# A two-layer block with GELU on one core: when transposes and stores are given out on SP's queue

## The chip, the cores and the metric

The kernel runs on one core of a Trainium2 chip. The metric is the time of one execution on the device in microseconds (us), lower is better. Before: 1465.05 us, the median of three runs (1464.21 to 1468.51).

## The reference

```python
# x: (8, 1024, 1024) float32, w1: (1024, 4096), w2: (4096, 1024)
h = x @ w1
h = 0.5 * h * (1 + np.tanh(np.sqrt(2 / np.pi) * (h + 0.044715 * h ** 3)))
return (h @ w2).astype(np.float32)
```

## The kernel before

**Tiling.** The 8192 rows of x are taken in eight token blocks of 1024 rows (`sb` 0 to 7). Each runs a first multiplication (x by w1, GELU on ScalarE, result g) and a second (g by w2, result to `out`). Both are split into 2 x 2 blocks, named "11", "12", "21", "22", and are done with seven products in place of eight (the scheme of Strassen and Winograd): products 1, 2 and 3 take blocks of the weights as they are, 5, 6, 7 and 4 take sums of them (`W1_SUM`, `W_SUM`, listed in `SUMS`), and sums of x or g stand on the other side (`X_SUM`, and the jobs `g`). From block 2 on, a second level of the same scheme is used inside the products. Data are float16, accumulation is in float32 in PSUM.

**The stage in question** is the second multiplication of token block 0, `matmul2_made(0, ...)`. It computes what the later blocks will load ready-made, and stores it to DRAM: the four blocks of w2 (`keep`, into `w2_d`, shown as `w_d` in the profile), and for each operand m the sums that the second level needs (`split_jobs`, into `in_d[m]`). Its products run in the order 1, 2, 5, 6, 3, 7, 4, each in four quarters of 128 rows (sixteen matmuls each); product 3 is done with the second level, in seven steps.

**The order by hand.** After each quarter, `run((m, q))` looks into the table `FILL[0]` and does the jobs written there. The key `60` stands for product 6, quarter 0, and so on; `31` to `37` are the seven steps of product 3. The jobs: `g` sums of g; `wmn` piece n of the sum of w2 for product m (`make`); `pmn` the split sum n of operand m with its store to `in_d[m]`; `a` the inner sums of g; `x` and `q` the sums of x and of w1 for the next token block; `i` inner sums of w1. VectorE does them in this order, in between the sums that empty PSUM (`post`).

**Queues.** Most loads, and some stores, are issued on SP's queue (`nc.sync`, and `load_in_order`, which also fixes their place in the program's order); other stores, and copies that cast, are issued by POOL. Each queue issues in order: what stands first and waits holds up what stands behind it. A DMA of SP's queue also starts only when the eighth before it on that queue has landed.

**The next block's x.** During product 5, POOL starts eight copies of the next 1024 rows of x from float32 to float16 in DRAM (`x_cast`, buffer `xb`). `x_transpose` loads from that buffer with the transposing DMA into four tiles, in the order "22", "21", "12", "11", four transposes for each; SP's queue waits for the cast to land. `x_blocks` takes the four tiles.

**Who waits for what.** Tiles `u` come from a pool of 24, tiles `mu` from one of two, `gc` from one of four. The split sums p35 and p36 of operand 3 lie in `u` tiles, p37 and p34 in the two `mu` tiles. p25, p26, p27 and p24 of operand 2, which VectorE makes from the end of product 3 on, take the place of some of these once those have been read by TensorE and stored. Product 4 needs the sums w40 to w43, which come behind p27 and p24 on VectorE. The first multiplication of block 1 begins with the raw blocks of w1 that `MadeQuad(0, False, True)` loads, and with the transposed x.

In the profile, L1127 is the second level's matmul in the second multiplication, L1182 the one of a plain product there, L502 that of a plain product in the first, L719 that of the second level there. L142 is VectorE's addition or subtraction, L169 ScalarE's copy, L166 a DMA given out by `load_in_order`, L203 a load of w1's raw blocks, L836 and L848 stores of results, L1010 the store of a split sum.

Of the kernel before, what the change touches and what calls it, by code (L numbers as in the profile page):

```python
# [23 lines left out]
SUMS = tuple(W_SUM)  # L24
# [19 lines left out]
def slots(table):  # L44
# [4 lines left out]
    slots("""10:g60 p15;11:g61 p16;12:g62 p17;13:g63  # L49
    ;20:g50 w50 w51;21:g51 w52;22:w53 g52;23:g53 p14  # L50
    ;50:w60 w61;51:w62 w63;52:g30 g31;53:g32 g33
    ;60:p35 p36;61:a35 p37;62:a37 p34;63:a36
    ;31:w70;32:a33;33:w71;34:w72;35:w73;36:p25;37:p26
    ;70:p27 p24;71:w40 w41;72:w42 w43;73:x5;40:x7;41:x6;42:x3 q5 q6 q7 q4
    ;43:i2""".replace("\n    ", "")),
# [21 lines left out]
def kernel(  # L77
# [7 lines left out]
    nc = tc.nc  # L85
# [38 lines left out]
    in_d = {m: dram.tile([P, 4, NI // 2, OH // 2], DT, name=f"in_d{m}") for m in range(1, 8)}  # L124
# [5 lines left out]
    term = {b: m for m, b in W_TERM.items()}  # L130
# [7 lines left out]
    def unit(rows, cols):  # L138
        return up.tile([P, rows, cols], DT, name="u")

    def tt(out, in0, in1, op, pin=False):
        i = nc.vector.tensor_tensor(out=out, in0=in0, in1=in1, op=op)  # L142
        if pin:
            tc.keep_in_program_order(i)

    def w1_at(q, key):
        for (at, ks), d in w1_d.items():
            if at == q and key in ks:
                return d[:, :, ks.index(key), :]

    def w2_at(q, m):
        return w2_d[q // 2, m][:, :, q % 2, :]

    def halves(t):
        return t.rearrange("p (h k) n -> p h (k n)", h=2)
# [9 lines left out]
    def load_in_order(out, in_, **kw):  # L165
        return tc.keep_in_program_order(nc.sync.dma_start(out=out, in_=in_, **kw))  # L166
# [26 lines left out]
    class MadeQuad:  # L193


        def __init__(self, q, first, store):
            self.q, self.first, self.store = q, first, store
            self.raw = {b: unit(2 * KH, 2 * P) for b in BLOCKS}
            self.ops = {m: self.raw[b] for m, b in W_TERM.items()}
            if not first:  # L200
                queue = nc.sync
                for b in ("12", "11", "22", "21") if q else ("11", "21", "12", "22"):
                    queue.dma_start(out=halves(self.raw[b]), in_=w1_at(q, term.get(b, b)))  # L203

        def load(self):

# [156 lines left out]
    def x_blocks():  # L363
        return {b: unit(KH, HT) for b in ("22", "21", "12", "11")}
# [107 lines left out]
    def x_cast(s, after, rows=range(0, SB, P), xb=None):  # L472
        if xb is None:
            xb = xdram.tile([SB, H], DT, name="xb")
        with tc.issue_after(after.ins):
            for q in rows:
                nc.gpsimd.dma_start(out=xb[q:q + P, :], in_=x2[s * SB + q:s * SB + q + P, :])
        return xb
# [8 lines left out]
    def x_transpose(xb, dma, blocks=None, which=range(4)):  # L487
        blocks = blocks or x_blocks()
        for b, t in [list(blocks.items())[i] for i in which]:
            a, k = int(b[0]) - 1, int(b[1]) - 1  # L490
            for j in range(KH):
                dma(
                    t[:, j, :],
                    xb[a * HT:(a + 1) * HT, (k * KH + j) * P:(k * KH + j + 1) * P],
                    transpose=True,
                )
        return blocks
# [343 lines left out]
        rows = out2[r0:r0 + HT // 2, o0:o0 + OH // 2].rearrange("(i p) n -> p i n", p=P)  # L841
        return nc.sync.dma_start(out=rows, in_=src)

    def store_rows(sb, o, a, src, **kw):
        r0 = sb * SB + (int(o[0]) - 1) * HT + a * HT // 2
        o0 = (int(o[1]) - 1) * OH
        rows = out2[r0:r0 + HT // 2, o0:o0 + OH].rearrange("(i p) n -> p i n", p=P)
        return nc.gpsimd.dma_start(out=rows, in_=src, **kw)  # L848

    def matmul2_made(sb, g, keep_w1, xb):  # L850

# [23 lines left out]
        def keep(b):  # L875
            if sb == 0:
                for q in range(NI // QC):
                    load_in_order(w2_at(q, term.get(b, b)), raw[b][q])
# [3 lines left out]
        def make(m, q):  # L882
            if m not in sums:
                sums[m] = raw[over[m]] if m in over else [unit(2, HALF) for _ in range(NI // QC)]
            u, op, v = W_SUM[m]
            in0, in1 = (sums[b][q] if isinstance(b, int) else raw[b][q] for b in (u, v))
            tt(sums[m][q], in0, in1, op, True)
            if sb:
                n = 1 if q < 2 else 2
                nc.gpsimd.dma_start(out=w2_at(q, m)[:, :n], in_=sums[m][q][:, :n])  # L890
# [4 lines left out]
        def rows(t, q):  # L895
            return t[:, :, q * P:(q + 1) * P]

        s2, a, p5, t6, at = {}, {}, {}, {}, {}
# [3 lines left out]
        deep = {m: Inner(m, g[operands[m]]) for m in ((3,), (4,))[sb]}  # L902
        for m, d in deep.items():
            d.base, d.y = [], parts[m]
            d.rows = lambda r, t, o={3: "12", 4: "21"}[m]: store_rows(sb, o, r, t)

        def run(key):
            for job in FILL[sb].get(key, ()):
                kind, m, n = job[0], int(job[1]), int(job[2:] or 0)
                if kind == "g" and m == 6:  # L910
                    s2[n] = gcp.tile([P, NI, P], GT, name="gc")
                    tt(s2[n], rows(g["22"], n), rows(g["21"], n), SUB, True)
                elif kind == "g" and m == 5:
                    tt(rows(g["11"], n), s2[n], rows(g["11"], n), ADD, True)
                elif kind == "g":
                    tt(rows(g["12"], n), rows(g["12"], n), s2[n], SUB, True)
                elif kind == "w":
                    make(m, n)
                elif kind == "p":
                    splits[m][SUMS.index(n)]()  # L920
                elif kind == "a":
                    deep[m].make(n)
                elif kind == "x":
                    xs.make(m, pin=True)
                elif kind == "q":
                    quad.sum(m, pin=True)
                elif kind == "i" and sb:
                    xs.make_inner(m)
                elif kind == "i":
                    quad.inner_sums(m)  # L930
# [31 lines left out]
        for m, name, first in (  # L962
            (1, "a", True), (2, "b", True), (5, "c", True), (6, "a", False),
            (3, "c", False), (7, "a", False), (4, "a", False),
        ):
            if m in deep:
                deep[m].pieces = pieces(m)
                for n in deep[m].steps(deep[m].base):
                    if (m, n) == (4, 1):
                        quad = StoredHalf(0)  # L970
                    run((m, n))
                continue
            for q in range(NQ):
                if first:
                    banks[name].append(psum())
                bank = banks[name][q]
                matmuls2(bank, s2[q] if m == 6 else rows(g[operands[m]], q), pieces(m), first)
                post(m, q, bank)
                if (m, q) == (5, 0) and sb == 0:
                    xb = x_cast(sb + 1, nc.gpsimd.tensor_copy(out=pace, in_=p5[0][:, :2]))  # L980
                if (m, q) == ((5, 0) if sb else (6, 0)):
                    xs = XOps(x_transpose(xb, load_in_order))
                if (m, q) == (6, 3):
                    keep("22")
                if (m, q) == (7, 0) and sb == 0:
                    quad = MadeQuad(0, False, True)
                if (m, q) == (1, NQ - 1) and sb == 0:
                    sums[5] = [unit(2, HALF) for _ in range(NI // QC)]
                    for t in sums[5]:
                        act_copy(t[:, 0, :1], warm)  # L990
                    bring("22", act_copy, True)
                    keep("21")
                    keep("12")
                run((m, q))
        return xs, [quad]

    def split_jobs(m, pieces, t):

        def operand(v, h):
            if isinstance(v, int):  # L1000
                return t[v][:, h * QC:(h + 1) * QC, :]
            k, b = int(v[0]) - 1, int(v[1]) - 1
            return chunks(pieces()[2 * k + h])[:, b]

        def make(n):
            u, op, v = W_SUM[n]
            t[n] = (mp.tile([P, NI // 2, OH // 2], DT, name="mu") if n in (7, 4) and m != 4 else unit(NI // 2, OH // 2))
            for h in range(2):
                tt(t[n][:, h * QC:(h + 1) * QC, :], operand(u, h), operand(v, h), op, True)
            (nc.sync if m == 3 else nc.gpsimd).dma_start(out=in_d[m][:, SUMS.index(n)], in_=t[n])  # L1010

        return [lambda n=n: make(n) for n in SUMS]

# [186 lines left out]
    def matmul2(sb, g, early, nxt):  # L1200
        end = sb == NSB - 1
        into = {}

        def out(o, **kw):
            return lambda a, t: store_rows(sb, o, a, t, **kw)

        operands = {1: "11", 2: "12", 5: "11", 6: "22", 7: "21", 3: "12"}
        products = {m: Inner(m, g[b]) for m, b in operands.items()}
# [72 lines left out]
    xs, quads = first.xs, [first.quad]  # L1281
    g_late = None
    for sb in range(NSB):
        if sb < 2:
            g, nxt = matmul1(xs, sb, quads, first if sb == 0 else None)
            xs, quads = matmul2_made(sb, g, None if sb else quads[-1].keep_raw, nxt)
# [3 lines left out]
        xs = nxt  # L1290
# [30 lines left out]
```

## Time and profile before

| | |
|---|---|
| median of three runs | 1465.05 us |
| profiled execution | 1467.82 us |
| its span in the trace | 1466.0 us |
| TensorE busy | 1449.4 us (99%) |
| VectorE busy | 1207.9 us (82%) |
| ScalarE busy | 712.2 us (49%) |
| POOL busy | 587.4 us (40%) |
| mean DMA rate | 314 GB/s |
| granted TensorE clock, mean | 0.997 |

The page's table in 40 slices of 36.65 us shows where the span is not full: the first slices cover block 0, whose stage in question lies from 112 to 218 us.

```
PE   9999979999999999999999999999999999999998
DVE  5657749858698898889898898988989889888887
PEclk9999989999999999999999999999999999999999
DMA  9999899898799999999999999999999999986594
```

The stretches below are taken from the trace, with the time that TensorE was busy, the mean share of time in which the 16 DMA engines were busy, and what they moved.

| from, to (us) | what runs on TensorE | TensorE busy (us) | DMA share | GB/s |
|---|---|---|---|---|
| 150.0 to 168.4 | products 5 and 6 | 18.40 of 18.40 | 1.03 | 280 |
| 168.4 to 193.4 | products 3 and 7 | 25.00 of 25.00 | 0.60 | 136 |
| 193.4 to 202.1 | nothing | 0.03 of 8.70 | 1.01 | 382 |
| 202.1 to 218.5 | product 4 | 16.37 of 16.40 | 1.02 | 367 |
| 218.5 to 275.0 | block 1, first multiplication | 56.20 of 56.50 | 0.98 | 364 |
| 275.0 to 280.0 | the same | 5.00 of 5.00 | 0.07 | 29 |

How to read the rows of the profile: a row of the timeline gives start, length, engine, line, operation, output and input tiles, and in brackets how long the engine had been idle before it and what released it. "SPq" is SP's queue of DMAs, and its lengths are those of issuing; a DMA lands later. A row of the stretches gives the stretch, its length, then the busy time of TensorE, its weight loads, VectorE, ScalarE and POOL with the number of instructions, and last the granted TensorE clock, the DMA share and GB/s. The chain of waits goes back from the last instruction to what released it each time.

### The profile page before, as it was taken

Reading aid. Unit: us, or ns where it says so; the run is one execution under the profiler, and the core shown is the slowest. Engines: PE = TensorE matmul, PEld = TensorE weight load, DVE = VectorE, ACT = ScalarE, POOL = GpSimd, SP = SyncE. Lnnn points to the kernel's source line nnn. Section 1 sums busy time; section 2 is a strip of 40 time slices with the busy share of each in tenths; the row PEclk is TensorE's granted clock in tenths of the full one; section 3 lists DMA queues with packets and bytes.
Section 4 is the critical chain, followed back from the end, with each engine's and each line's share of the span. In section 5 each row is a group of like instructions: output and inputs, shape, how many; then the busy total and the mean of one; then the engine's idle time right before and its main releaser. Section 6 shows DMA issues by size and latency. Waiting matters only on the chain.

```text
span 1466.0 us, 28909 instructions
## 1 busy us (share of the span) xinstructions
PE 1449.4 (99%) x10731; PEld 1049.3 (72%) x10731; DVE 1207.9 (82%) x2019; ACT 712.2 (49%) x1460; POOL 587.4 (40%) x602
## 2 busy tenths in 40 slices
PE   9999979999999999999999999999999999999998
PEld 5444634444577788778887788777887778877887
DVE  5657749858698898889898898988989889888887
ACT  5665105641158621785228841388225872268621
POOL 1542113222359500793018820388005960068400
PEclk9999989999999999999999999999999999999999
DMA  9999899898799999999999999999999999986594
GB/s 316 344 354 377 235 306 368 287 324 247 274 397 250 280 365 375 332 251 315 361 349 328 239 363 338 367 294 226 388 357 353 264 262 372 358 332 232 209 405 162
DMA packets 199116, 460.13 MB, mean 314 GB/s; under 512 B 75200, under 2 KB 80320, under 8 KB 198080
## 3 DMA queue, kind: packets, MB, share of 16 engines
q1 hardware_dynamic: 178208, 375.45, 74.5%
q0 software_dynamic: 20768, 82.85, 17.4%
q8 instruction: 84, 1.38, 0.4%
q14 instruction: 56, 0.46, 0.1%
HBM read 370.15 MB, written 102.76 MB: 323 GB/s over the span
## 4 chain that ended last, share of the span: by engine, by line
PE 96%; SPq 1%; DMA 1%; DVE 1%; issue 0%; ACT 0%; DVEq 0%
PE ps L1127 36%; PE ps L502 26%; PE ps L719 23%; PE ps L1182 11%; SPq L166 1%; PE ps L435 1%; DMA u<-in_d 1%; DVE u L142 0%; DMA u<-in_x_dram 0%; PE ps L412 0%; DMA in_d<-u 0%; DVE mu L142 0%; ACT u L169 0%; DVE tmp L142 0%; PE ps L370 0%
## 5 line engine op out<-in xcount | busy, mean ns | idle before, releaser
L169 ACT COPY tmp<-ps 128x512 f32<-128x512 f32 (+1 forms) x528 | 263.8, 540 | 238.9 <-PE ps L502 143.8
L502 PE MATMUL ps<-u 128*128 128x512 f16 x1472 | 343.2, 379 | 0.3 <-DVE tmp L142 0.3
L1127 PE MATMUL ps<-u,gc 128*128 128x256 f16 x2704 | 308.8, 273 | 0.8 <-DMA u<-in_d 0.8
L1127 PEld LDWEIGHTS <-gc 128*128 128x128 f16 x2816 | 275.5, 98 | 32.9 <-DMA u<-in_d 1.0
L142 DVE TENSOR_TENSOR u<-u 128x2048 f16<-128x2048 f16 (+3 forms) x292 | 221.9, 803 | 47.0 <-DMA in_d<-u 14.9
L142 DVE TENSOR_TENSOR tmp<-tmp,ps 128x256 f32<-128x256 f32 (+1 forms) x368 | 197.1, 544 | 71.5 <-PE ps L719 30.6
L719 PEld LDWEIGHTS <-u 128*128 128x128 f16 x2096 | 205.1, 98 | 57.3
L502 PEld LDWEIGHTS <-u 128*128 128x128 f16 x1472 | 144.1, 98 | 141.6 <-issue 0.9
L848 POOL DMA_DIRECT2D out_dram<-u x50 | 36.8, 735 | 515.5 <-DVE u L142 495.4
L1127 PE MATMUL ps<-u,g 128*128 128x256 f16 x2000 | 234.8, 273 | 0.0
L1127 PEld LDWEIGHTS <-g 128*128 128x128 f16 x2112 | 206.6, 98 | 24.3
L719 PE MATMUL ps<-u 128*128 128x256 f16 x1372 | 221.1, 273 | 0.0
L515 ACT ACTIVATE g<-tmp 128x512 f16<-128x512 f32 x282 | 174.2, 641 | 57.5 <-DVE tmp L142 56.6
L169 ACT COPY ps<-ps 128x256 f32<-128x256 f32 (+1 forms) x208 | 95.4, 458 | 219.3 <-PE ps L1127 219.3
L142 DVE TENSOR_TENSOR ps<-tmp,ps 128x256 f32<-128x256 f32 x444 | 181.5, 426 | 17.3 <-PE ps L719 9.4
L169 ACT COPY u<-ps 128x512 f32<-128x512 f32 (+1 forms) x114 | 66.2, 587 | 180.7 <-PE ps L1127 146.9
L142 DVE TENSOR_TENSOR u<-u,ps 128x512 f32<-128x512 f32 x174 | 118.5, 684 | 40.9 <-ACT u L169 20.9
L1182 PE MATMUL ps<-u,g 128*128 128x512 f16 x640 | 141.5, 384 | 8.7 <-DVE u L142 8.7
L515 ACT ACTIVATE g<-ps 128x512 f16<-128x512 f32 x230 | 137.9, 601 | 24.7 <-PE ps L719 15.2
L771 POOL TENSOR_TENSOR tmp<-tmp 128x512 f32<-128x512 f32 x96 | 122.2, 1275 | 41.8 <-DVE tmp L142 31.5
L142 DVE TENSOR_TENSOR tmp<-ps,tmp 128x512 f32<-128x512 f32 x126 | 86.6, 690 | 48.1 <-PE ps L502 40.3
L1182 PEld LDWEIGHTS <-g 128*128 128x128 f16 x640 | 63.2, 99 | 86.1 <-issue 12.5
(72 smaller groups left out, 1572.3 us busy)
## 6 DMA issues: line engine op xcount, KB each, us to landing
u<-w_d SPq DMA_DIRECT2D x347, 512.0 KB, 8.9
u<-in_d SPq DMA_DIRECT2D x162, 512.0 KB, 9.3
out_dram<-u POOLq DMA_DIRECT2D x50, 512.0 KB, 6.9
gc<-in_w_dram SPq DMA_DIRECT2D x48, 512.0 KB, 6.5
g<-w_d SPq DMA_DIRECT2D x45, 512.0 KB, 7.8
w_d<-u POOLq DMA_DIRECT2D x40, 512.0 KB, 6.3
w_d<-u SPq DMA_DIRECT2D x32, 512.0 KB, 9.4
xb<-in_x_dram POOLq DMA_DIRECT2D x56, 256.0 KB, 7.1
```

What stands on the lines that cost most here:

```text
L142: i = nc.vector.tensor_tensor(out=out, in0=in0, in1=in1, op=op)
L166: return tc.keep_in_program_order(nc.sync.dma_start(out=out, in_=in_, **kw))
L169: tc.keep_in_program_order(nc.scalar.copy(out=out, in_=in_))
L435: tc.keep_in_program_order(nc.tensor.matmul(bank[:, cols], lhsT=w[:, k, :], rhs=self.xs.blocks[f"{a}{r}"][:, k, cols], start=r == 1 and k ...
L502: tc.keep_in_program_order(nc.tensor.matmul(bank, lhsT=w, rhs=x, start=first and k == 0, stop=k == n - 1, skip_group_check=not first,))
L515: gelu_last[0] = nc.scalar.activation(out=out, in_=src, func=GELU, scale=scale)
L719: tc.keep_in_program_order(nc.tensor.matmul(out, lhsT=w, rhs=x, start=first and k == 0, stop=k == 1, skip_group_check=not first,))
L771: tc.keep_in_program_order(nc.gpsimd.tensor_tensor(out=t, in0=t, in1=temp("p", m), op=ADD))
L848: return nc.gpsimd.dma_start(out=rows, in_=src, **kw)
L1127: tc.keep_in_program_order(nc.tensor.matmul(bank[:, i * OH // 2:(i + 1) * OH // 2], lhsT=t[:, c, i * P:(i + 1) * P], rhs=self.weights(j, c ...
L1182: tc.keep_in_program_order(nc.tensor.matmul(pair(bank), lhsT=a[:, c, :], rhs=chunks(pieces[c // QC])[:, :, c % QC, :], start=(first and c ...
```

## The change

Six edits, all of them in the order of DMAs or the queue that issues them:

- the transposes of the next block's x, given out in one go after the first quarter of product 6, are given out four at a time by a new job `t` after each of its quarters (in block 1's stage they stay together);
- block "22" of w2 is stored after the last quarter of product 5 and no longer after the last of product 6;
- the stores of split sums of operand 3 are fixed in the program's order, and those of operand 2 move from POOL's queue to SP's, fixed as well;
- the two row stores of product 3's result "12" in block 0 move from POOL's queue to SP's, fixed in order;
- the loads of the first four raw blocks of w1 for block 1 are fixed in order;
- arguments that are no longer used go.

```diff
-    ;60:p35 p36;61:a35 p37;62:a37 p34;63:a36
+    ;60:p35 p36 t0;61:a35 p37 t1;62:a37 p34 t2;63:t3 a36
...
-                    queue.dma_start(out=halves(self.raw[b]), in_=w1_at(q, term.get(b, b)))
+                    (queue.dma_start if q else load_in_order)(out=halves(self.raw[b]), in_=w1_at(q, term.get(b, b)))
...
-    def store_rows(sb, o, a, src, **kw):
+    def store_rows(sb, o, a, src, start=nc.gpsimd.dma_start):
...
-        return nc.gpsimd.dma_start(out=rows, in_=src, **kw)
+        return start(out=rows, in_=src)
...
-            d.rows = lambda r, t, o={3: "12", 4: "21"}[m]: store_rows(sb, o, r, t)
+            d.rows = lambda r, t, o={3: "12", 4: "21"}[m], q=load_in_order if m == 3 else nc.gpsimd.dma_start: store_rows(sb, o, r, t, q)
...
+                elif kind == "t":
+                    x_transpose(xb, load_in_order, xs.blocks, (m,))
...
+                if (m, q) == (5, 3):
+                    keep("22")
                 if (m, q) == ((5, 0) if sb else (6, 0)):
-                    xs = XOps(x_transpose(xb, load_in_order))
-                if (m, q) == (6, 3):
-                    keep("22")
+                    xs = XOps(x_transpose(xb, load_in_order, which=range(4 if sb else 0)))
...
-            (nc.sync if m == 3 else nc.gpsimd).dma_start(out=in_d[m][:, SUMS.index(n)], in_=t[n])
+            (load_in_order if m in (2, 3) else nc.gpsimd.dma_start)(out=in_d[m][:, SUMS.index(n)], in_=t[n])
```

In the built program SP's queue then stands, from the stores of block "12" of w2 on: four stores of block "22"; the stores of p35 and p36; four transposes ("22"); the store of p37; four transposes ("21"); the store of p34; eight transposes ("12", "11"); a row store, the store of p25, a row store, the store of p26; the loads of raw "11", "21", "12", "22" of w1; the stores of p27 and p24. Before it stood: sixteen transposes; the stores of p35, p36, p37 and p34; four stores of block "22"; the loads. TensorE, VectorE and ScalarE have the same instructions in the same order in both.

More of the change, by code (lines that the diff above doesn't have):

```diff
@@ L1202, in matmul2, with out @@
         into = {}
-        def out(o, **kw):
-            return lambda a, t: store_rows(sb, o, a, t, **kw)
+        def out(o):
+            return lambda a, t: store_rows(sb, o, a, t)
         operands = {1: "11", 2: "12", 5: "11", 6: "22", 7: "21", 3: "12"}
```

## The prediction

> **What bounds the kernel now.** The page gives TensorE 1449.4 us of the 1466.0 us span, so the question is where its 16.6 us of idling lie. I read the waits by engine first: one gap of TensorE is over 1.2 us, L1182 waiting once for VectorE. Then the timeline of TensorE around it (start, length, instruction, idle before and what ended it):
>
> ```profile
> 179.45 13.98 PE L1182 MATMUL ps<-u,g 128*128 128x512 f16 x64
> 202.13 16.55 PE L1182 MATMUL ps<-u,g 128*128 128x512 f16 x64 [8.70 <-DVE u L142]
> 218.52 16.74 PE L502 MATMUL ps<-u 128*128 128x512 f16 x76
> ```
>
> The first row is product 7 of token block 0, the second product 4, the third the start of token block 1. TensorE stands from 193.43 to 202.13. The stretches of that time show the granted clock (last but two columns):
>
> ```profile
> 193.40:197.00 3.60, 0.03 (x1) 0.00 (x0) 2.76 (x5) 0.00 (x0) 1.11 (x2) 1.00 1.01 401
> 197.00:202.10 5.10, 0.00 (x0) 0.00 (x0) 5.10 (x9) 0.00 (x0) 2.88 (x6) 0.51 1.01 368
> 202.10:207.40 5.30, 5.27 (x13) 1.87 (x13) 5.30 (x6) 0.00 (x0) 0.97 (x2) 0.50 1.02 379
> 207.40:218.50 11.10, 11.10 (x53) 4.98 (x51) 4.09 (x4) 1.76 (x3) 0.66 (x2) 1.00 1.02 361
> ```
>
> The clock is halved 3.6 us after TensorE stops and comes back 5.3 us after it resumes, so product 4 takes 16.55 us where product 7, equally large, took 13.98. The chain of waits tells why VectorE was late:
>
> ```profile
> 189.91 1.26 SPq L166
> 191.27 2.95 DMA in_d<-u
> 194.24 1.36 DVE u L142 x3
> ...
> 200.86 1.23 DVE u L142
> 202.13 16.55 PE ps L1182 x64
> ```
>
> and the timeline of VectorE and SP's queue what those rows are:
>
> ```profile
> 194.24 1.29 DVE L142 TENSOR_TENSOR u<-u 128x1024 f16<-128x1024 f16 x2 [14.87 <-DMA in_d<-u]
> ...
> 168.44 22.73 SPq L166 DMA_TRANSPOSE u<-xb  x16
> 191.27 1.00 SPq L1010 DMA_DIRECT2D in_d<-u  x2
> 192.36 2.08 SPq L1010 DMA_DIRECT2D in_d<-mu  x2
> 194.48 5.42 SPq L166 DMA_DIRECT2D w_d<-u  x4
> 200.08 16.93 SPq L203 DMA_DIRECT2D u<-w_d  x8
> ```
>
> VectorE's job p25 writes the buffer that p35 held, and p35 may go only when its store to in_d has landed. p35 was made at 158, but its store stands on SP's queue behind sixteen transposes, which wait until 168.4 for the cast of x and then take 22.73 us to issue. So p25 runs at 194.24 in place of 179.4, and p26, p27, p24, w40 follow it in VectorE's order; product 4 needs w40.
>
> **The change, part by part.** Its arithmetic is the same; the built programs have the same instructions in the same order on TensorE, VectorE and ScalarE. Only SP's queue and POOL's differ.
>
> *Block "22" of w2 (keep) goes ahead of product 6.* Four stores, issue 5.42 us in all. They are ready at 148.7 (ScalarE's last cast) and follow the stores of "12", whose last issue ends at 151.5, onto a ring that already has a backlog: those four were issued at 146.1 to 150.1 and landed 20.3 to 20.5 us later, at 166.4 to 170.6. So the new four land at about 172 to 176.1, by the steps of 1.3 to 1.4 us in which 512 KB copies land there. Can they delay the cast of x, for which the transposes wait? From 157 to 166 the two queues moved
>
> ```profile
> q0 software_dynamic: 212, 1.74, 92.8%
> q1 hardware_dynamic: 214, 0.41, 12.6%
> ```
>
> (packets, MB, share of the engines): one packet of SP's queue for each of the cast's, however long SP's backlog. It lasted beyond the cast (168.3), so more of it takes nothing more; I take zero. The other bound is that the 2.1 MB come first, 4 x 1.35 = 5.4 us.
>
> *p35 and p36 are stored ahead of the transposes, p37 and p34 between them.* The built program lets each DMA of SP's queue start only when the eighth before it has landed, so p35's store starts at 166.4 and p36's at 167.7. They land behind block "22", near 177.5 and 178.9. p25 is due at 179.4 and needs p35 alone (p26 needs a store of block "22", 172). The wait of 14.87 us goes to 0; at worst 1 to 2 us stay.
>
> *Sixteen transposes in fours.* The first starts at 169.2 (it waits for "12"'s third store) in place of 168.44. Issue cost stays 22.73 / 16 = 1.42 us. In the ring they follow p36, so the first four land at about 179.7 to 182; when there was a backlog, at 329.4 to 334.8, eight landed in steps of 0.8 us. p37 lands at 183.5, the next four by 186.7, p34 at 188. p27 wants p37's buffer at 183.6, p24 wants p34's at 184.9: some 3 us of wait for VectorE. Behind p24 stand the sum of product 7's second quarter, w40 to w43 (1.2 us each) and two sums of 0.68: w40 ends at 191.2, w41 192.3, w42 194.2, w43 195.4. TensorE asks for them at 193.43, 194.3, 195.2 and 196.0 (a quarter of 13.98 is one pass of four weights' pieces, a sixteenth 0.87). Covered, by 0.6 us at the tightest. If transposes land in copies' steps of 1.35, p34 lands at 192.5 and some 4 us of the gap stay.
>
> *Two row stores and the four stores of p2 move from POOL's queue to SP's; raw loads of the next block are pinned behind two of them.* POOL's queue waited up to 25.8 us at L848 and now has only the sums of product 7, which come free earlier; nothing on it gets later. On SP's queue the last transpose is issued at about 169.2 + 22.7 + 2.0 (p37, p34) = 193.9, four stores at about 0.5 each end at 196, and the loads of raw "11", "21", "12", "22" follow by 198. They land behind four stores at 1.35 each and the transposes' tail (195): "11" at 201.8, "21" 203.1, "12" 204.5, "22" 205.8; with two of POOL's 256 KB stores in turn, 1.3 later. VectorE's x5, x7, x6, x3 wait for these four stores and the last transpose and end at about 202. Token block 1 starts at 193.43 + 13.98 = 207.4 and needs "11"; product 5 needs the difference of "11" and "12" (1.22 us on VectorE) 3.4 us later, at 210.9. Slack 4 to 5 us.
>
> *Does the DMA have room?* From 168.4 to 193.4 its share was 0.60, ten idle us of all engines; the eight stores moved into that time take 8 x 1.35 = 10.8. The stretch from 193.4 on, full before (1.01 to 1.02), is relieved of as much as TensorE gains, and it ended in slack (share 0.07 from 275 to 280). So nothing is owed later.
>
> **Sum.** 8.70 us of gap and 16.55 - 13.98 = 2.57 us of half clock: 11.3 us. The profiled execution took 1467.82 us, so 1456.5; the median shown, 1465.05, is 2.8 below it, so **1453.8 us**. The half clock goes only if the rest of the gap stays under 3.6 us. The Trainium skill (TensorE: Matmul & The Clock Gate, Part 1) puts both the idling that closes the clock gate and the work that opens it at about 3.4 us. By that the half clock cost 1.7 us and the time would be 1454.7; the rows (3.6 closed, 5.3 to open) decide.
>
> **Rivals.**
> *A part of the gap stays* (p34 late, or "12" late at product 5). For it: only 0.6 us of cover before w43, and transposes interleaved with copies landed 5.9 to 6.7 us after issue from 322 on, against 2.9 here. Against: SP's eight places absorb that. Price up to 4 us, below the 3.6 that halve the clock or just at it: 1457.8.
> *The gap moves to the start of token block 1.* The pace of SP's queue is now the whole question, since the raw loads stand behind all of it. At 1.8 us per transpose the last is issued at 169.2 + 28.8 + 2.3 = 200.3, four stores at 1.37 (the w_d stores' issue under load) end at 205.8, "11" lands 9.9 later (the median of such loads from 193.4 to 218.5) at 215.7, and 2.6 us of half clock follow: 218.3 in place of 218.52. No change, 1464.8.
> *Slower, by the same mechanism further on.* Two of the sixteen transposes took 2.05 and 2.17 us to issue. If the full ring makes all do so: 169.2 + 16 x 2.17 + 2.3 = 206.2, stores to 211.7, "11" at 221.6, TensorE idle since 210, half clock 2.6: 224.2 against 218.5, 1470.8. It decides from the point where "11" lands after 215.9. Against it: with copies among them, from 462.5 to 485.4, seventeen DMAs of that queue still went at 1.43 us each.
>
> **How the numbers follow.** Forecast 0.60, part of the gap 0.22, no change 0.09, slower 0.09. A measurement here can tell about 0.3% (4.4 us) from nothing: the first two are faster, 0.82; 0.09 the same; 0.09 slower. The range runs from 1450.5 (the forecast, less 0.8, as far as the fastest run shown lies under its median, and less half of the 5.0 us that TensorE still idles after 399, 1062.03 busy of 1067.00) to 1462.5 (a gap that keeps 8.7 us of its 11.3) and leaves out most of the last two cases. The likeliest's own range is 1452 to 1456.
>
> **What would show it.** Right: no gap of TensorE between products 7 and 4 over 1 us and no half clock after the first 20 us; p25 at about 179.4 to 181; in_d stores landing before 190; loads of raw "11" issued by 198 and block 1 at 207.4. The cast's landing at 168.3 shows the packet argument right; 173 shows it wrong. Wrong: TensorE waiting at the start of block 1 for u<-w_d, or transposes issued in steps of 1.8 us and more.

## The result, and the profile after

The changed kernel takes 1460.15 us (median of 7 runs, 1457.87 to 1464.41); the kernel before, on the same chip, 1466.03 (7 runs, 1464.21 to 1469.64). The ratio is 0.9958, 95% interval 0.9942 to 0.9975: faster by 0.4%. The profiled execution took 1460.05 us, its span 1458.3 (before 1467.82 and 1466.0).

The timeline of TensorE after the change, from product 7 on (start, length, instruction; in brackets the idle time before it and what ended it):

```profile
180.21 27.79 PE L1184 MATMUL ps<-u,g 128*128 128x512 f16 x128
209.31 3.63 PE L502 MATMUL ps<-u 128*128 128x512 f16 x16 [1.32 <-DMA u<-w_d]
213.54 8.81 PE L502 MATMUL ps<-u 128*128 128x512 f16 x40 [0.60 <-DVE u L142]
223.29 24.69 PE L502 MATMUL ps<-u 128*128 128x512 f16 x112 [0.95 <-DVE tmp L142]
248.91 11.38 PE L502 MATMUL ps<-u 128*128 128x512 f16 x52 [0.93 <-DVE tmp L142]
```

The first row is products 7 and 4 in one piece, 27.79 us for two of 13.98 less their overlap: the gap of 8.70 us and the half clock are gone. But token block 1 (L502) now opens with four gaps, 3.80 us in all, the first for a raw block of w1, the others for VectorE. Before, the same stretch had one gap over 0.25 us:

```profile
255.40 4.91 PE L502 MATMUL ps<-u 128*128 128x512 f16 x22 [0.29 <-DVE tmp L142]
```

The timeline of VectorE shows its waits in that time, each longer wait on a DMA:

```profile
189.39 1.29 DVE L142 TENSOR_TENSOR mu<-u 128x1024 f16<-128x1024 f16 x2 [3.57 <-DMA in_d<-mu]
201.51 5.00 DVE L142 TENSOR_TENSOR u<-u 128x2048 f16<-128x2048 f16 x4 [4.50 <-DMA out_dram<-u]
212.26 6.25 DVE L142 TENSOR_TENSOR u<-u 128x2048 f16<-128x2048 f16 x8 [5.74 <-DMA u<-w_d]
246.70 1.56 DVE L142 TENSOR_TENSOR u<-u 128x512 f16<-128x512 f16 x4 [2.22 <-DMA w_d<-u]
```

The first is p24 (it waits for p34's store), the second the sums of x, the third q5, the first sum of w1 for block 1, which needs raw "11" and "12". The last is an inner sum of w1 whose buffer is held by an earlier inner sum until POOL's store of that one has landed. In the kernel before, the same two instructions, q5 and that inner sum, stood here:

```profile
219.72 6.27 DVE L142 TENSOR_TENSOR u<-u 128x2048 f16<-128x2048 f16 x8 [8.13 <-DMA u<-w_d]
253.19 1.56 DVE L142 TENSOR_TENSOR u<-u 128x512 f16<-128x512 f16 x4 [1.22 <-DMA w_d<-u]
```

SP's queue after the change (lengths are those of issuing):

```profile
170.25 8.73 SPq L166 DMA_TRANSPOSE u<-xb  x4
...
185.99 11.86 SPq L166 DMA_TRANSPOSE u<-xb  x8
...
201.59 4.12 SPq L166 DMA_DIRECT2D u<-w_d  x4
```

The last transpose is issued by 197.85; the raw loads follow four stores and start at 201.59. Their landings, by the semaphores in the trace: "11" at 209.27, "21" 210.70, "12" 212.18, "22" 213.46. Each took 7.5 to 8.3 us from its issue to its landing, at a time when the DMA engines were full. These are stretches of the changed kernel (start:end, length, busy time of TensorE, weight loads, VectorE, ScalarE, POOL, then granted clock, DMA share, GB/s):

```profile
168.40:180.00 11.60, 11.60 (x109) 10.40 (x108) 10.50 (x12) 1.14 (x2) 0.00 (x0) 1.00 1.13 347
180.00:200.00 20.00, 20.00 (x96) 9.17 (x94) 12.65 (x18) 0.59 (x1) 2.76 (x5) 1.00 0.84 200
200.00:246.00 46.00, 43.08 (x198) 19.02 (x196) 36.72 (x64) 21.30 (x39) 13.18 (x20) 1.00 1.01 375
```

From 200 to 246 they are full; while the transposes run, from 180 to 200, they move only 200 GB/s at a share of 0.84.

Last, the chain of waits through block 1's opening:

```profile
238.58 8.09 DMA w_d<-u
246.67 0.02 issue
246.70 0.44 DVE u L142
...
248.17 0.70 DVE tmp L142
248.87 0.04 issue
248.91 13.11 PE ps L502 x60
```

It goes from the landing of a store of w1's sums over VectorE's inner sum to TensorE, where it went over VectorE's w40 and product 4 before.

### The profile page after: what moved, and what is told of

It is laid out like the page before. It is cut to its first block, busy times and chain, and to the rows that moved or that the text cites. A ratio compares the mean times of both kernels' runs of the same rounds, so it can differ in the third digit from the quotient of the medians.

```text
span 1458.3 us, 28912 instructions
## 1 busy us (share of the span) xinstructions
PE 1447.5 (99%) x10731; PEld 1048.6 (72%) x10731; DVE 1210.6 (83%) x2019; ACT 711.6 (49%) x1460; POOL 583.1 (40%) x596
## 4 chain that ended last, share of the span: by engine, by line
PE 85%; DMA 8%; issue 4%; POOL 1%; DVE 1%; ACT 0%; SPq 0%; POOLq 0%; DVEq 0%
PE ps L1129 36%; PE ps L719 23%; PE ps L502 19%; PE ps L1184 6%; DMA gc<-in_w_dram 3%; DMA u<-in_w_dram 2%; DMA w_d<-u 1%; PE ps L435 1%; POOL u L172 1%; DMA xb<-in_x_dram 1%; DVE u L142 0%; PE ps L412 0%; SPq L166 0%; ACT u L169 0%; DMA u<-in_x_dram 0%
## 5 line engine op out<-in xcount | busy, mean ns | idle before, releaser
L502 PE MATMUL ps<-u 128*128 128x512 f16 x1472 | 343.8, 379 | 4.4 <-DVE tmp L142 1.9
L502 PEld LDWEIGHTS <-u 128*128 128x128 f16 x1472 | 143.8, 98 | 146.8 <-issue 3.0
```

What stands on the lines that cost most here:

```text
L502: tc.keep_in_program_order(nc.tensor.matmul(bank, lhsT=w, rhs=x, start=first and k == 0, stop=k == n - 1, skip_group_check=not first,))
```

## The experiments

Ten kernels were run. One measure is used throughout, the **stage**: from the first matmul of product 3 to the first matmul of block 1's second multiplication. It took 148.60 us before and takes 141.36 after. (The expectations of the first four runs count it from product 6 and to the end of the first multiplication, 14.0 us more: 162.58 and 155.33.) Taking away every gap and the half clock of the kernel before would leave 148.60 - 8.70 - 2.57 - 0.29 = 137.04. Diffs are against the changed kernel unless another is named. The ratio of each is to the kernel before on the same chip.

| run | time (us) | ratio, interval | stage (us) |
|---|---|---|---|
| the change | 1460.15 | 0.9958 [0.9942, 0.9975] | 141.36 |
| e1_burst_behind | 1459.68 | 0.9947 [0.9931, 0.9962] | 140.94 |
| e2_rows_p2_pool | 1462.05 | 0.9962 [0.9949, 0.9976] | 143.87 |
| e3_block22_late | 1460.58 | 0.9951 [0.9938, 0.9965] | 140.94 |
| e4_parts_alone | 1460.43 | 0.9951 [0.9937, 0.9964] | 141.34 |
| e6_12_second | 1460.21 | 0.9950 [0.9934, 0.9967] | 139.88 |
| e7_p2_late | 1458.43 | 0.9938 [0.9919, 0.9956] | 137.61 |
| e8_both | 1459.12 | 0.9948 [0.9931, 0.9965] | 141.01 |
| e9_burst_order_alone | 1457.66 | 0.9938 [0.9916, 0.9959] | 138.89 |
| e10_order_p2_late | 1455.57 | 0.9924 [0.9911, 0.9937] | 137.62 |
| e11_more_vector | 1465.03 | 0.9987 [0.9976, 0.9999] | 145.72 |

### Which edit removes the gap: e1 to e4

e1 puts the sixteen transposes back into one burst, behind the four stores of operand 3:

```diff
-    ;60:p35 p36 t0;61:a35 p37 t1;62:a37 p34 t2;63:t3 a36
+    ;60:p35 p36;61:a35 p37;62:a37 p34;63:t0 t1 t2 t3 a36
```

> Stage = from the first matmul of product 6 to the first matmul of block 1's second multiplication: 162.58 us before (315.99 - 153.41), 155.33 after (309.50 - 154.17). Theory Q (order on SP's queue): what pays is that the stores of p35, p36, p37 and p34 stand ahead of the transposes, not that these are given out in parts. One burst behind the four stores then does as well: no gap between products 7 and 4, stage 154.5 to 157, time within 2 us of the changed kernel's 1460.2. Rival P (the parts pay): the transposes start later and end 4 us or more later than 197.9, raw "11" lands at 213 or later, stage 159 or more, 1464 or more.

No gap came back between products 7 and 4, and the stage is 0.4 us shorter than with the change. So it is the order, stores ahead of transposes, that pays; the four parts are not needed for it. The gaps in block 1 stayed, 3.46 us in all (gaps over 0.25 us are counted).

e2 gives the row stores of "12" and the stores of operand 2 back to POOL's queue:

```diff
-            d.rows = lambda r, t, o={3: "12", 4: "21"}[m], q=load_in_order if m == 3 else nc.gpsimd.dma_start: store_rows(sb, o, r, t, q)
+            d.rows = lambda r, t, o={3: "12", 4: "21"}[m]: store_rows(sb, o, r, t)
...
-            (load_in_order if m in (2, 3) else nc.gpsimd.dma_start)(out=in_d[m][:, SUMS.index(n)], in_=t[n])
+            (load_in_order if m == 3 else nc.gpsimd.dma_start)(out=in_d[m][:, SUMS.index(n)], in_=t[n])
```

> The two row stores of "12" and the stores of p2 back on POOL's queue, all else as changed. Theory Q: the 3.8 us that TensorE now waits in block 1 (1.32 + 0.60 + 0.95 + 0.93) come from the raw loads standing behind four stores on SP's queue; without these, raw "11" lands by 204 in place of 209.3, the waits fall to 0.3, stage 151.5 to 152.5, time 3 to 4 us under the changed kernel's 1460.2, so 1456 to 1457. Rival B (bandwidth): the engines have the same bytes to move before the loads whichever queue they stand on; "11" lands at 207 or later, stage 154.5 to 156, time unchanged.

The gap is back, in part (4.58 us), and with it the half clock (product 4 takes 16.55 us again). Neither theory had foreseen it; raw "11" landed at 207.38, as Rival B said. TensorE's and VectorE's timelines of e2:

```profile
198.72 16.55 PE L1184 MATMUL ps<-u,g 128*128 128x512 f16 x64 [4.58 <-DVE u L142]
```

```profile
195.64 1.29 DVE L142 TENSOR_TENSOR mu<-u 128x1024 f16<-128x1024 f16 x2 [9.87 <-DMA in_d<-mu]
```

It is p24 again: POOL's six stores went beside the transposes, these took longer (the second four landed by 193.05, with the change by 186.69), and p34's store, which stands behind them, landed at 195.55 instead of 189.29. With the transposes in parts, p34 is exposed to whatever slows eight of them. Block 1, entered at 215.11, had no gap.

e3 stores block "22" after product 6 again; e4 does so too and has e2's edit as well, so that of the change only the parts, the order and the pinned loads are left:

```diff
-                if (m, q) == (5, 3):
-                    keep("22")
...
+                if (m, q) == (6, 3):
+                    keep("22")
```

> Block "22" stored where it was, after the last quarter of product 6, which is now between the third and the last four transposes. Theory Q: its four stores (5.4 us) stand ahead of the raw loads again; the first four transposes go faster (5.7 us in place of 8.73), so the net is raw "11" 2 to 3 us later than 209.3, stage 157 to 158.5, time 1462 to 1463. Rival R (the backlog of "22" is what made the transposes late): the transposes end at 195 or earlier but for these stores, "11" lands by 207, stage 153 or less, time 1458 or less.

> Only the parts and the pinned stores of p3 are kept: block "22" stored late, rows and p2 on POOL's queue. Theory Q: on SP's queue the raw loads stand behind four stores in place of four others, so about as the changed kernel: no gap between products 7 and 4, stage 154 to 156.5, time 1459 to 1461.5. Rival R: stage 152 or less. Rival P is not touched by it.

Both are as fast as the change within its interval, with no gap between products 7 and 4. e4 came out as its Theory Q said; e3 lies between its two theories, and raw "11" landed there at 207.51, earlier than with the change (209.27), not later. Block "22" early brings nothing on its own, and without it ahead of them the stores of operand 3 are early enough for e2's edit to do no harm: in e4 p24 doesn't wait at all. In all four kernels raw "12" landed between 210.2 and 211.6, whatever stood where; and in all but e2 block 1 opened with gaps of 3.4 to 4.1 us. So what the change lacked to the forecast had to be looked for there.

### What holds block 1: e6 to e8

Two limits were suspected: the landing of raw "12", from which VectorE starts, and the landing of the store before the inner sum at 246. e6, against e1, loads raw "12" ahead of "21":

```diff
-                for b in ("12", "11", "22", "21") if q else ("11", "21", "12", "22"):
+                for b in ("12", "11", "22", "21") if q else ("11", "12", "21", "22"):
```

> The burst stands behind the four stores of operand 3 (as in e1_burst_behind), and raw "12" is loaded ahead of raw "21". Measure: the stage, from the first matmul of product 3 to the first matmul of block 1's second multiplication (before 148.60 us, after 141.36, e1_burst_behind 140.94). Theory V (VectorE's start on the sums of w1 sets the pace of block 1): q5 starts at 209.0 in place of 210.32, all that follows on VectorE moves with it, the gaps of TensorE at 220 and 228 (0.95 and 0.44) go and the stage takes 139.6. Theory B (the DMA engines are full from 200 on, and the store of a sum of w1 lands at 246.3 to 246.7 whatever stands before it, 246.28 in e1_burst_behind and 246.70 in the changed kernel): q5 is earlier as well and the early gaps shrink, but VectorE's wait at 246 grows from 3.76 to about 5, the gap there from 2.07 to about 3.4, and the stage stays at 140.9. Time 1458.4 by V, 1459.7 by B.

e7, against e1, gives out the stores of p27 and p24 (1 MB) only behind the loads of w1's fourth quarter:

```diff
+            dst = in_d[m][:, SUMS.index(n)]
+            if m == 2 and n in (7, 4):
+                owed.append((dst, t[n]))
+            else:
+                (load_in_order if m in (2, 3) else nc.gpsimd.dma_start)(out=dst, in_=t[n])
...
                 quads.append(quad)
+                if sb == 1 and q == 2:
+                    for dst, src in owed:
+                        load_in_order(dst, src)
```

> As e1_burst_behind, but the stores of p27 and p24 (two of 512 KB, which there stand between the loads of w1's first and second quarter) follow the loads of its fourth quarter, where the DMA engines have little to do (share 0.03 from 270 to 275 in the changed kernel). Theory B: 1 MB less is ahead of the store that VectorE waits for at 246.28, at some 390 GB/s 2.7 us; it lands at about 243.6, the wait of 3.76 falls to about 1, the gap of TensorE of 2.07 goes, and the stage takes about 139 (e1_burst_behind 140.94). Theory V: q5 does not move (210.3), so the gaps of 0.95 and 0.44 stay, and the stage stays at 140.5 to 141. Time 1457.7 by B, 1459.7 by V.

> Both edits: raw "12" second, the stores of p27 and p24 behind the fourth quarter of w1. If the two limits stand one behind the other (V until 245, then B), only both together bring the whole: no gap of TensorE over 0.5 us in block 1, stage 137.5 to 138.3 (e1_burst_behind 140.94 less 3.46 of gaps at most), time about 1456.5 to 1457.2. If V alone holds it equals e6_12_second, if B alone e7_p2_late.

e6 fell between its two expectations: q5 at 209.26 (but q6 then waited 1.37 us for raw "22"), wait at the inner sum 2.69, stage 139.88. It settles little, for another reason as well: e1, e6, e7 and e8 have the same SP queue up to raw "11", and yet p34's store landed there at 180.21, 180.21, 179.40 and 181.79, and raw "11" at 207.62, 207.94, 206.92 and 209.58. Single traces differ by up to 2.7 us in these landings with no edit at all. e8 drew the latest of them; its gaps at 207.78 and 211.52 (1.84 and 0.92) come from that, and it doesn't answer its question.

The trace of e7 shows a stage of 137.61, where about 139 was the better of its two expectations; its median, 1458.43, lies between the two (1457.7 and 1459.7). VectorE's timeline of e7:

```profile
209.60 1.22 DVE L142 TENSOR_TENSOR u<-u 128x2048 f16<-128x2048 f16 x1 [5.06 <-DMA u<-w_d]
...
242.74 1.55 DVE L142 TENSOR_TENSOR u<-u 128x512 f16<-128x512 f16 x4 [0.78 <-DMA w_d<-u]
```

The wait before the inner sum fell from 3.76 in e1 to 0.78, and of TensorE's gaps one of 0.89 was left. From q5 to the inner sum it is 33.14 us, in e1 35.96: 2.8 us for 1 MB, and this difference lies within each trace, so it does not hang on when raw "12" landed. (From e6 to e8, which differ by the same edit, the wait falls by less, from 2.69 to 1.39.) So in both pairs of traces these 512 KB stores were in the way; the times alone don't show it, since the intervals of e7 and e1 overlap.

**The chain, over all runs.** Where VectorE waits before that inner sum (in all but e2 and e11), its start and the start of the second multiplication keep one distance:

| run | q5 starts | wait for the store | inner sum starts | second multiplication | difference |
|---|---|---|---|---|---|
| before | 219.72 | 1.22 | 253.19 | 315.83 | 62.64 |
| after | 212.26 | 2.22 | 246.70 | 309.34 | 62.64 |
| e1 | 210.32 | 3.76 | 246.28 | 308.92 | 62.64 |
| e3 | 210.38 | 2.93 | 245.78 | 308.42 | 62.64 |
| e4 | 211.68 | 2.03 | 246.31 | 308.95 | 62.64 |
| e6 | 209.26 | 2.69 | 245.47 | 308.11 | 62.64 |
| e7 | 209.60 | 0.78 | 242.74 | 305.38 | 62.64 |
| e8 | 211.10 | 1.39 | 246.13 | 308.78 | 62.65 |
| e9 | 210.08 | 1.22 | 243.50 | 306.13 | 62.63 |
| e10 | 209.34 | 0.89 | 242.43 | 305.06 | 62.63 |

(In e7 and e10 no gap of TensorE over 0.25 us follows that wait; there VectorE and TensorE come out even.) Between q5 and the wait VectorE works: 253.19 - 219.72 - 1.22 = 32.25 us before, 32.22 after, 32.20 in e1. It had no slack even in the kernel before: TensorE entered block 1 at 218.52, q5 started 1.2 us later, and one gap of 0.29 us followed. An earlier start of TensorE is worth no more than what q5, and the wait for the store behind it, gain.

### Is VectorE without slack? e11

e11 lets VectorE make q4, which TensorE needs only in the pair's last product, four times more before the sum that counts (the result is the same):

```diff
-    ;70:p27 p24;71:w40 w41;72:w42 w43;73:x5;40:x7;41:x6;42:x3 q5 q6 q7 q4
+    ;70:p27 p24;71:w40 w41;72:w42 w43;73:x5;40:x7;41:x6;42:x3 q5 q6 q7 e4 e4 e4 e4 q4
...
+                elif kind == "e":
+                    quad.ops.setdefault(m, None)
+                    quad.ops[m] = quad.ops[m] or unit(2 * KH, 2 * P)
+                    u, op, v = W1_SUM[m]
+                    tt(quad.ops[m], *((quad.ops if isinstance(b, int) else quad.raw)[b] for b in (u, v)), op, True)
```

> The changed kernel with four more passes of VectorE over the sum q4 ahead of the one that counts (4 x 1.22 = 4.88 us; the tile and its one store are the same). TensorE needs q4 only in the last product of that pair, so nothing waits for it directly. Theory C (VectorE has no slack between q5 and the inner sum at 246.70): the inner sum starts 4.88 later less what its wait of 2.22 gives up (it was never under 0.78), at 250.1 to 251.6, TensorE's gaps grow by as much, the second multiplication starts 62.64 after it, stage 144.8 to 146.2, time 1463.5 to 1465. Rival S (VectorE has spare time there, and only the landing of the raw blocks delayed product 5): TensorE's gaps stay within 1 us of those of the changed kernel (3.80 in all), stage 141 to 142.4, 1460 to 1461.5.

VectorE's and TensorE's timelines of e11:

```profile
211.40 11.30 DVE L142 TENSOR_TENSOR u<-u 128x2048 f16<-128x2048 f16 x12 [5.24 <-DMA u<-w_d]
```

```profile
227.48 34.87 PE L502 MATMUL ps<-u 128*128 128x512 f16 x152 [5.99 <-DVE tmp L142]
```

The 5.05 us more of VectorE (11.30 against 6.25) stand as a gap of TensorE of 5.99 where the change had 0.95. Up to there nothing was absorbed. The gap halved the clock until 231.4, 3.9 us beyond its end, which adds half of that, 1.9 us, and the time went to 1465.03, near that of the kernel before.

Further on a part was absorbed. The wait of 2.22 us before the inner sum is gone: that sum starts at 249.48, 2.8 us later than with the change (Theory C said 250.1 to 251.6), and the second multiplication follows it by 64.51 us, not 62.64. The stage, 145.72, lies where Theory C put it and the time at its upper end, but partly by luck: 1.9 us of both are the half clock, which it left out. So VectorE is the bound of block 1's opening up to that wait; from there on the landing of the store has a say.

### The order alone, and a faster version: e9, e10

e9 is the kernel before with the one order that e1 showed to pay (e1's burst, e2's and e3's edits on top; the pinned loads stay):

> The kernel before with a single edit of effect: the sixteen transposes in one burst behind the stores of p35, p36, p37 and p34 (block "22" is stored late, row stores and operand 2 on POOL's queue as before). Theory Q (that order alone removes the gap of 8.70 and its half clock): no gap between products 7 and 4 over 1 us, stage 141 to 142 as in the changed kernel, 1459.5 to 1460.5. Rival: the other edits carry a part, since POOL's stores alternate with the transposes as in e2_rows_p2_pool: a gap of 1 to 4 us there, stage 143 to 146, 1462 to 1464.

The burst then stands behind the stores of operand 3 and of block "22", and in this one place the queue's order differs from the kernel before. The gap is gone, at 1457.66 us: less than both theories said, and the other edits aren't needed for it. Its interval overlaps that of the change, so it isn't shown to be faster; its stage is 2.5 us shorter, in one trace. e10 adds e7's edit to e9:

> As e9_burst_order_alone, but the stores of p27 and p24 follow the loads of w1's fourth quarter (as in e7_p2_late). Measure: the stage, from the first matmul of product 3 to the first matmul of block 1's second multiplication (before 148.60 us, after 141.36, e9 138.89, e7 137.61); without any gap of TensorE it would be 148.60 - 8.70 - 2.57 - 0.29 = 137.04. Theory C (a chain sets the stage: raw "12" lands, VectorE starts q5, works 32.2 us without a pause, waits for the store of a sum of w1, and 62.64 us after that the second multiplication starts; both the landing and the last wait hang on the bytes ahead on the DMA engines): 1 MB less on POOL's queue beside the transposes, so these end at 200 to 201 in place of 203.05, raw "12" lands at 207.5 to 208.5 in place of 209.96, VectorE's wait is 0.8 to 1.2, no gap over 0.6, stage 137.0 to 137.6, 1456 to 1457.5. Rival R (SP's pace of issuing sets the landing, 1.3 us a transpose, whatever the bytes): raw "12" stays at 209.5 to 210, the wait of 1.22 goes to 0.8, stage 138.4 to 138.9, 1457.5 to 1458.

TensorE's timeline of e10:

```profile
179.67 27.79 PE L1192 MATMUL ps<-u,g 128*128 128x512 f16 x128
207.30 12.25 PE L503 MATMUL ps<-u 128*128 128x512 f16 x56
220.35 41.93 PE L503 MATMUL ps<-u 128*128 128x512 f16 x193 [0.80 <-DVE tmp L142]
```

One gap of 0.80 is left, the stage is 137.62, and the time, 1455.57 (1454.59 to 1457.35), beats both kernels: its interval, 0.9911 to 0.9937, lies below that of the change. The stretches of e10 show where the room came from:

```profile
180.00:200.00 20.00, 20.00 (x95) 9.05 (x93) 13.44 (x18) 0.59 (x1) 5.19 (x9) 1.00 1.07 265
200.00:246.00 46.00, 45.20 (x210) 20.34 (x209) 39.03 (x71) 22.68 (x42) 13.85 (x21) 1.00 0.95 344
```

Beside the transposes the engines move 265 GB/s where the changed kernel moved 200: 1.3 MB more in 20 us, since POOL's queue puts its stores between them (3.41 MB of POOL's queue for 1.05). The transposes did end later (landed 202.45, in the changed kernel 200.04): their issue took 27.25 us, where it took 27.60 with two stores among them, but it began 3.15 us later, at 173.40. Raw "12" gained less than Theory C said, 209.22 after 209.96 in e9, which is nearer to Rival R; the stage and the time are Theory C's. And the 46 us after that are no longer full, 0.95 for 1.01.

## Why the prediction was right, and where it was wrong

**How near it came.** The time, 1460.15 us, lies inside the range (1450.5 to 1462.5) but outside the likeliest's own (1452 to 1456): 5.9 us were gained where 11.3 were forecast. That the range holds it is in part luck. Its upper end was made for a gap between products 7 and 4 that stays, and that gap went whole; what was lost was lost later, and mostly to a chain that the prediction didn't have.

**Right: what bounds, and that it goes.** The gap of 8.70 and the half clock of 2.57 vanished, by the mechanism named: p25 ran at 180.04 (forecast 179.4 to 181), p34's store landed at 189.3 (188), p24 waited 3.57 (some 3), and its cover held. That block "22" wouldn't delay the cast held too: it landed at 170.10, not 168.3, but it was issued 2.0 us later; from its first issue to its last landing it took 18.1 us, in the kernel before 18.3. (Its first issue varies without block "22" ahead as well: 148.9 in e9, 152.1 in e10, 152.0 after the change.)

**Wrong: "Slack 4 to 5 us."** This step gave the loads of raw w1 by 198 and q5 in good time. Measured against it:

| | forecast | after |
|---|---|---|
| last transpose issued | 193.9 | 197.85 |
| raw loads issued | by 198 | 201.59 to 205.7 |
| raw "11", "12" land | 201.8, 204.5 | 209.27, 212.18 |
| q5 starts | in time for 210.9 | 212.26 |

Half of the delay is the issue: the first transpose started 1.05 us late, right behind the cast's landing, and the first four took 8.73 us, not 4 x 1.42 = 5.7; the other twelve kept 1.44. The other half is landing: from the end of the last transpose's issue to raw "11" 11.4 us in place of 7.9. The four stores ahead landed 1.4 to 2.8 us apart, not 1.35; one store of POOL's lies between them, and from 205 to 210 the engines were busy throughout (share 1.00) at 292 GB/s, for which no run gives the reason.

**The deeper error in the same step** is what q5 was measured against. It asked whether q5 comes before product 5 needs it. But VectorE works 32.2 us without a pause from q5 on, and then waits for a store; with q5 as late after TensorE's start as before (1.2 us) there is one gap of 0.29, with 4.27 (212.26 against 207.99) there are four. The sum counted what TensorE gains at product 4, 11.27 us; the stage could only gain what VectorE's chain gained. That is 219.72 - 212.26 = 7.46 at q5, less 1.00 by which the wait for the store grew, 6.49 at the inner sum with rounding; with product 3 starting 0.75 later in that execution (0.52 of it from a wait of TensorE at 36.7, long before the change), the stage is 7.24 shorter. Of 11.27, then, 4.03 was given back in block 1.

**Wrong as well: "So nothing is owed later."** The bytes were owed: e7 moved 1 MB out of the full stretch, and the path from q5 to the inner sum shortened by 2.8 us (by 1.2 from e6 to e8). The share of 0.07 from 275 to 280 in the kernel before was slack, but behind the point that counted.

**The rest of the miss.** Of the 6.3 us missed, 4.0 are block 1's. Another 1.0 is the start: the forecast stood on a median of three runs, 1465.05, and seven runs of the kernel before give 1466.03. The last 1.4 stay open: between the two traces the stage shortened by 7.24 us, and the medians differ by 5.9, while the runs of one kernel spread over 5.4 us before and 6.5 after.

**A bound that doesn't hold.** The prediction kept the half clock away from any gap under 3.6 us, in the sum and in the price of the first rival. It cost nothing here, since the gap went whole. But e8's wait of 2.38 us in block 2 halved the clock (see the last section).

**The rivals.** The nearest was "A part of the gap stays", with its clause "or "12" late at product 5" and up to 4 us: its price is what was measured, though product 5's own wait is just 0.60 and the rest goes by VectorE. "The gap moves to the start of token block 1" and "Slower" needed transposes at 1.8 and 2.17 us each throughout; only the first four came at that pace.

**Left open.** A wait of TensorE in block 2, near 495 to 508, for loads of in_d or a sum made of them: 0.76 us before, none after, 0.79 in e3, 1.31 in e4, 1.65 in e7, 2.38 in e8, 0.34 in e11, none in e9 and e10. It was not tried what sets it; the two longest came where the stores of p27 and p24 go late, but e10, which does the same, had none. Nor was it tried to give the inner sum at 246 a buffer of its own, another way to take its wait away.

## What to carry to other kernels

When a gap is closed, look for the engine that used it to catch up: the credit is the smallest slack on every chain that runs through the gap, counted to the end of that chain, and not to its next meeting with TensorE. Here an instruction some 40 us further on, with the same distance of 62.64 us to the next stage in trace after trace, showed which chain counted. A queue should hold first what frees buffers, then what fills them in bulk; and stores that nobody waits for belong beside slow transfers or behind the full stretch, not among the loads, provided that no store that is waited for stands behind those transfers, as p34's did in e2.

## What the runs showed of the hardware

Transposes behind the stores of block "22" and of operand 3 were dear to issue: the first four took 8.73 us in the changed kernel and 7.0 to 9.1 in every other trace with that order, against 5.57 and 5.83 in e3 and e4, where block "22" isn't ahead of them. The other twelve of the changed kernel took 1.44 each. With POOL's stores beside them the issue could be dear as well: one group of four took 11.52 us in e4. While the transposes were given out the DMA engines moved 136 GB/s before (168.4 to 193.4), 200 with the change and 265 in e10 (both from 180 to 200), where another queue had stores to put between.

The clock didn't keep one delay. Before, it was halved 3.7 us after TensorE stopped and was back 5.3 us after it resumed; in e2 3.0 and 5.3 us, in e11 3.0 and 3.9 us. In e8 a shorter stop was enough. These are TensorE's rows of block 2 in e7 and in e8:

```profile
496.89 5.49 PE L1137 MATMUL ps<-u,gc 128*128 128x256 f16 x48 [1.65 <-DVE gc L142]
```

```profile
501.02 7.07 PE L1137 MATMUL ps<-u,gc 128*128 128x256 f16 x48 [2.38 <-DMA u<-in_d]
```

The same 48 matmuls took 5.49 us behind the wait of 1.65 and 7.07 behind that of 2.38, where the clock was halved 2.6 us after TensorE stopped, 0.2 us after it had resumed, and back 3.6 us after it resumed. The Trainium skill (TensorE: Matmul & The Clock Gate, Part 1) gives about 3.4 us for both and says that the window of the monitor runs freely, so that this varies from run to run; the closings lie around that figure, the openings above it. In the four traces' records of the clock, the half clock lasted 10.24 us (before), 6.83 (e2 and e11) and 3.41 (e8), and the full clock ahead of it 187.73, 187.73, 215.04 and 491.52: all are whole multiples of 3.413 us. So the clock changed on a grid of that step, and the length of a stop alone didn't tell its price: stops of 8.70 and 4.58 us both cost product 4 its 2.57, one of 5.99 cost 1.9.
